# A two-layer hybrid block: gates worked in the product's PSUM bank, output weights split by two other engines, the last weights split during the attention

## The chip, the cores and the metric

The kernel runs on one core of one Trainium2 chip. The metric is the device time of one execution in microseconds, the median of three runs. Engines: PE (TensorE, matmuls), DVE (VectorE), ACT (ScalarE), POOL (GpSimd) and SP (SyncE, which issues most of the DMAs). Each engine works through its own instructions in program order and waits for other engines by semaphores.

## The reference, cut to what matters

Two layers run over 1280 tokens (1024 latent and 256 context) of width 1024, all in fp32. Layer 0 is the part around the first two edits, layer 1's last product the part around the last.

```python
def _ab_mixer(h, ...):                                   # layer 0
    z = h @ w_in
    a, ga, u, v, gb = jnp.split(z, [...])                # 512 columns each
    ya = _multiscale_pool(a, ...) * jax.nn.silu(ga)
    yb = _chunk_sgu(u, v, ...) * jax.nn.silu(gb)
    return jnp.concatenate([ya, yb], axis=-1) @ w_out    # "output product"
x = _layer_norm(ALPHA * x + gate * y, g, b)              # gate = row of silu(c) @ w_mod
...
def _cd_out(f_in, f_gate, attn, d_gate, fnet_w, w_out):  # layer 1
    yc = _fourier_mix(f_in, fnet_w) * jax.nn.silu(f_gate)
    yd = attn * jax.nn.silu(d_gate)                      # attn: 8 heads, 1024 queries, 1280 keys
    return jnp.concatenate([yc, yd], axis=-1) @ w_out    # last product
```

## The kernel before

**Products.** An fp32 operand is kept as two float32r parts, a high one (the value cast) and a low one (value minus high). `split` (L95 on) makes them: the cast is line 106, the subtraction line 107, and its arguments name the engine of each ("s" ACT, "v" DVE, "p" POOL). A product is three matmuls: high·high, high·low, low·high.

**Weights.** `Weights.fetch` loads a weight matrix in pieces of 128x1024 through staging tiles named raw (three buffers, shared with the rows of the modulation weights, rawmm and rawmg, and with other loads) and splits each piece. Without an `eng` entry the cast is DVE's and the subtraction POOL's.

**Order of the program.** A list of deferred work, ordered by a modelled clock, is looked into after each product (`defer`, `tick`, `spread`, `flush`). What is due is written into the program there; `pin` keeps an instruction where it was written. So a change of due times or of a clock moves instructions on every engine.

**Layer 0's gates.** The stages run: pooling input a, its gate ga, v, u, gate gb, output product. The tokens come in three segments (512, 512 and 256 wide). In `t_group`, each product of the gates stands in one of four PSUM banks (tile ps_mm); `ev_ga` and `ev_g` empty it: ACT writes silu of the bank into an SBUF tile (tag h32, two buffers, shared with the temporary tiles of the weighted sums), and DVE multiplies that with y in the tiles S (S5, S6, S7). Beside gb, three weighted sums over the modulation matrix are built: for each of eight rows one load, a DVE multiply-add for the latent row (acc, line 507) and for every second step ACT and POOL for the context row (lines 510 and 511). The last of them gives the gate rows: ps_g (line 530) sums acc over the partitions on PE, and line 532 adds the bias row brg. In the same stretch the first three pieces of the output weights, o0 to o2, are loaded and split (wH_o and wL_o, and wo).

**Output product.** After gb the list is flushed, then `y_split` splits the first two token tiles of y into yhl (the first by DVE alone, the second with POOL), and `y_mm` runs 24 matmuls 128x512 for each tile and half of the columns (ps_o, line 450).

**Attention and the last product.** Eight heads of four blocks follow a string of letters that orders pieces of score products (s), softmax, transposes (pt_p, copied to pT) and value products (av). Letters X take the next piece of a side list: among them `z_step`, which splits the last weights z0 and z1 in pieces 128x512 (cast ACT, subtraction POOL), and `z_piece`, three matmuls of the last product for the first two token tiles. After the attention the other two, z2 and z3, are fetched and split (tile wz), then the gate row and the normalisation vectors are loaded, and the last product (ps_z, line 450) and the final norm run.

```python
sl = hp.tile([P, 512], F32, tag="h32", name="sl", bufs=2)                             # ev_g, L736
nc.scalar.activation(sl[:, :n], ps, AF.Silu)
nc.vector.tensor_mul(y, sl[:, :n].rearrange("p (t c) -> p t c", c=P), y)
```

Of the kernel before, what the change touches and what calls it, by code (L numbers as in the profile page):

```python
# [50 lines left out]
def _body(nc, tc, A, ctx):  # L51
# [429 lines left out]
    for n in range(4):  # L481
        W.add(f"o{n}", halves_of(A["ab_w_out"], n // 2 * 512)[n % 2], 4, 512, eng=(None, None, None, ("s", "v"))[n])
# [146 lines left out]
    for ch in (1, 0):  # L629
        wh, wl = W.use(f"a{ch}")  # L630
        if ch == 1:
            aux(A["ab_pool_w"].rearrange("(g c) d -> c g d", c=P), 4, P, pwH, pwL, "pw")
        pads = [pp.tile([P, PADW], F32, tag="pad", name=f"pad{ch}"), spare[:, 0:PADW]]
        for pd in pads:
            for a0 in (0, 8 + S, PADW - 8):
                nc.gpsimd.memset(pd[:, a0:a0 + 8], 0.0)

        def ev_a(sg, j, ps, pads=pads):
            nc.scalar.copy(pads[j][:, OFF[sg]:OFF[sg] + SEG[sg][1]], ps)

# [12 lines left out]
        def ev_ga(sg, j, ps, ch=ch):  # L653
            g = 2 * ch + j
            y, pv, n = y_of(sg, g), ps.rearrange("p (t c) -> p t c", c=P), SEG[sg][1]
            if (sg, g) in half_done:
                sl = hp.tile([P, 512], F32, tag="h32", name="slg", bufs=2)[:, :n]
                nc.scalar.activation(sl, ps, AF.Silu)
                nc.vector.tensor_mul(y, sl.rearrange("p (t c) -> p t c", c=P), y)
            else:  # L660
                nc.scalar.activation(y, pv, AF.Silu)
            half_done.add((sg, g))

        t_group(wh, wl, h0, K0, ev_ga)
# [4 lines left out]
    sv = pool("sv", stack=st1)  # L669
# [4 lines left out]
    acc2 = sv.tile([P, 2, D], F32, name="acc2")  # L674
# [37 lines left out]
    def ev_v(t, ps):  # L712
# [8 lines left out]
           3.5, 12.0)  # L721
    for ch in range(2):
        wh, wl = W.use(f"u{ch}")

        def ev_u(sg, j, ps, ch=ch):
            y = y_of(sg, 4 + 2 * ch + j)
            pin(nc.vector.tensor_mul(y, ps.rearrange("p (t c) -> p t c", c=P), y))

        t_group(wh, wl, h0, K0, ev_u)
    for ch in range(2):  # L730
        wh, wl = W.use(f"gb{ch}")

# [82 lines left out]
    yh = {0: y_split(0), 1: y_split(1)}  # L815
    ps_of = {}
    for t in range(NT):
        src = A["x"][t * P:(t + 1) * P, :] if t < NL else A["ctx"][(t - NL) * P:(t - NL + 1) * P, :]
        if t == 0:
# [8 lines left out]
            wo.append(W.use("o3", ahead=False))  # L828
        xt = wp.tile([P, D], F32, tag="raw", name=f"xr{t}", bufs=3)
# [278 lines left out]
    def q_piece(hd, qq):  # L1108
# [64 lines left out]
    st5 = ExitStack()  # L1173
    ap_ = pool("ap", side="right", stack=st5)
# [76 lines left out]
    def s_piece(i, j):  # L1251
# [174 lines left out]
    yz, st_f = dict(enumerate(tail["y"])), tail["stack"]  # L1426
# [158 lines left out]
```

## Time and profile before

| what | value |
|---|---|
| time, median of 3 runs | 1096.69 us (1096.38 to 1096.76) |
| profiled execution: its own time | 1095.3 us |
| its span | 1093.5 us |
| mean granted clock | 0.992 of full speed |
| PE busy | 1061.9 us (97%) |
| DVE / ACT / POOL busy | 746.5 / 482.3 / 514.5 us (68 / 44 / 47%) |

The span is what the trace covers; 1.8 us of the profiled execution lie around it. Busy times of PE overlap each other by the pipeline, so what PE loses is seen in its idle stretches, and in the granted clock, which the page gives as a share of full speed.

### The profile page before, as it was taken

To read this page: it belongs to the slowest core of one execution; us is meant where nothing else is said; L and a number is where in the kernel's file an instruction comes from. 1 tells how busy PE (TensorE), PEld (TensorE's weight loads), DVE (VectorE), ACT (ScalarE), POOL (GpSimd) and SP (SyncE) were. 2 spreads that over 40 slices of the span, in tenths; PEclk is the share of its full clock that TensorE was granted. 3 is DMA by queue.
4 is the path that set the end of the run, shared out by engine and by line. 5 is a ranking of instruction groups with operands and counts; after the bars stand their busy time and mean duration, and the time that the engine had idled before them with its cause. 6 is when DMAs were issued, how large, how long until landed. Compare 5 with 4: busy or idle time off the path is not lost.

```text
span 1093.5 us, 16754 instructions
## 1 busy us (share of the span) xinstructions
PE 1061.9 (97%) x6082; PEld 912.0 (83%) x6082; DVE 746.5 (68%) x1664; ACT 482.3 (44%) x1145; POOL 514.5 (47%) x457
## 2 busy tenths in 40 slices
PE   8999999999988999999999999999999999999996
PEld 6888888888866888898888887889989989897886
DVE  3672646789986666777220056898999989894776
ACT  3511234523311333542021144788888888995010
POOL 3561401354482343122293125675655664875872
PEclk9999999999998999999999999999999999999999
DMA  9720110245442322502322010000000002014221
GB/s 365 248 76 29 49 58 1 78 140 184 141 165 90 109 97 93 153 1 92 121 77 77 25 58 29 2 1 1 1 1 1 1 1 59 20 59 153 98 102 73
DMA packets 39059, 85.61 MB, mean 78 GB/s; under 512 B 3056, under 2 KB 17520, under 8 KB 38080
## 3 DMA queue, kind: packets, MB, share of 16 engines
q1 hardware_dynamic: 36160, 76.60, 21.5%
q0 software_dynamic: 1664, 5.84, 1.4%
q10 hardware_dynamic: 1152, 2.10, 0.5%
q8 instruction: 48, 0.79, 0.3%
q14 instruction: 35, 0.29, 0.1%
HBM read 76.13 MB, written 8.39 MB: 77 GB/s over the span
## 4 chain that ended last, share of the span: by engine, by line
PE 73%; DVE 14%; DMA 4%; ACT 3%; issue 3%; POOL 3%; SPq 0%; DVEq 0%; POOLq 0%; ACTq 0%
PE ps_mm L210 16%; PE ps_o L450 10%; PE s L1106 8%; PE ps_n L450 8%; PE ps_z L450 7%; PE av L1324 5%; PE pt_p L1299 5%; DVE acc L507 3%; PE acc L362 2%; PE ps_y L1059 2%; PE ps_c L210 2%; PE pq L1116 1%; DVE S L507 1%; DVE mx L1265 1%; DMA rawmm<-in_cd_w_mod 1%
## 5 line engine op out<-in xcount | busy, mean ns | idle before, releaser
L1106 PE MATMUL s<-kT,qT 96*128 96x512 f32 (+1 forms) x576 | 147.8, 370 | 2.7 <-ACT p L1277 1.6
L1277 ACT ACTIVATE p<-s,mx 128x512 f32<-128x512 f32 (+1 forms) x192 | 119.0, 625 | 13.4 <-DVE mx L1288 12.5
L1265 DVE TENSOR_REDUCE mx<-s 128x1 f32<-128x512 f32 (+1 forms) x192 | 112.2, 595 | 10.6 <-PE s L1106 8.6
L1308 DVE TENSOR_TENSOR pT<-pt_p,pT 128x512 fp32r<-128x512 f32 x160 | 108.2, 684 | 11.4 <-ACT pT L1304 9.2
L1285 POOL TENSOR_SCALAR p<-p,mx 128x1280 f32<-128x1280 f32 x64 | 85.6, 1341 | 39.9 <-ACT pT L1304 11.2
L1106 PEld LDWEIGHTS s<-kT,qT 96*128 96x128 f32 x576 | 90.7, 189 | 15.5 <-ACT p L1277 5.3
L1304 ACT CAST pT<-pt_p 128x512 fp32r<-128x512 f32 x160 | 92.8, 588 | 19.1 <-PE pt_p L1299 11.9
L1299 PE MATMUL pt_p<-ident,p 128*128 128x128 f32 x640 | 93.0, 273 | 0.9 <-DVE kT L1212 0.5
L1299 PEld LDWEIGHTS pt_p<-ident,p 128*128 128x128 f32 x640 | 74.4, 140 | 7.6 <-ACT q L1122 1.1
L1324 PE MATMUL av<-pT,V 128*128 128x256 f32 x480 | 78.6, 291 | 0.1
L1324 PEld LDWEIGHTS av<-pT,V 128*128 128x128 f32 x480 | 67.5, 189 | 4.5 <-DVE pT L1308 0.3
L450 PE MATMUL ps_o<-wH_o,yhl 128*128 128x512 f32 x160 | 55.9, 411 | 6.0 <-DVE yhl L106 5.6
L450 PE MATMUL ps_o<-wo,yhl 128*128 128x512 f32 x240 | 57.5, 392 | 0.0
L450 PEld LDWEIGHTS ps_o<-wo,yhl 128*128 128x128 f32 x240 | 45.1, 189 | 9.2
L450 PE MATMUL ps_n<-wH_v,h 128*128 128x512 f32 x160 | 52.6, 397 | 0.0
L210 PE MATMUL ps_mm<-h,wH_u 128*128 128x512 f32 (+1 forms) x192 | 51.9, 358 | 0.0
L210 PE MATMUL ps_mm<-h,wH_gb 128*128 128x512 f32 (+1 forms) x192 | 51.6, 357 | 0.0
L210 PE MATMUL ps_mm<-h,wH_ga 128*128 128x512 f32 (+1 forms) x192 | 51.2, 354 | 0.0
L710 POOL TENSOR_TENSOR S<-S,bsb 128x256 f32<-128x256 f32 x20 | 18.3, 921 | 66.5 <-DVE S L709 66.5
L450 PE MATMUL ps_z<-wz,yz 128*128 128x512 f32 (+1 forms) x216 | 45.4, 367 | 2.5 <-POOL wz L107 2.5
L450 PEld LDWEIGHTS ps_z<-wz,yz 128*128 128x128 f32 x216 | 37.2, 188 | 9.7 <-POOL wz L107 2.9
L107 POOL TENSOR_TENSOR yhl<-S,yhl 128x1024 fp32r<-128x1024 f32 x9 | 23.5, 2609 | 40.4 <-DVE yhl L106 40.4
(394 smaller groups left out, 2832.8 us busy)
## 6 DMA issues: line engine op xcount, KB each, us to landing
rawmm<-in_cd_w_mod SPq DMA_DIRECT2D x16, 512.0 KB, 3.6
wm<-in_mod SPq DMA_DIRECT2D x7, 1024.0 KB, 9.0
rawmg<-in_ab_w_mod SPq DMA_DIRECT2D x8, 512.0 KB, 3.6
raw_o<-in_ab_w_out SPq DMA_DIRECT2D x8, 512.0 KB, 3.7
xr<-in_x SPq DMA_DIRECT2D x8, 512.0 KB, 3.6
xn_d<-S POOLq DMA_DIRECT2D x8, 512.0 KB, 2.9
rawmg<-in_cd_w_mod SPq DMA_DIRECT2D x8, 512.0 KB, 4.5
raw_z<-in_cd_w_out SPq DMA_DIRECT2D x8, 512.0 KB, 3.8
```

The source lines that it names most:

```text
L107: keep((nc.gpsimd if l == "p" else nc.vector).tensor_sub(dL, src, _f(dH)))
L210: nc.tensor.matmul(out, lhsT=a, rhs=b, start=(i == 0), stop=(i == n - 1))
L450: nc.tensor.matmul(ps, lhsT=lhsT(a, kk), rhs=w[b][:, k, :], start=(kk + i == 0), stop=(kk == KT - 1 and i == 2))
L507: pin(nc.vector.scalar_tensor_tensor(o, raw[:, c], s, o, op0=ALU.mult, op1=ALU.add))
L1106: pin(nc.tensor.matmul(out, lhsT=a, rhs=b, start=(i == 0), stop=(i == 2)))
L1265: pin(nc.vector.tensor_reduce(out=mx[:, j:j + 1], in_=ps, axis=AX.X, op=ALU.max))
L1277: pin(nc.scalar.activation(p32[:, e0:e0 + en], sc[e], AF.Exp, bias=mx[:, 3:4], scale=1.0, accum_out=mx[:, 4 + e:5 + e]))
L1285: pin(nc.gpsimd.tensor_scalar(p32, p32, mx[:, 8:9], 1.0, op0=ALU.mult, op1=ALU.mult))
L1299: pin(nc.tensor.transpose(pt[:, kk * 256 + i * P:kk * 256 + (i + 1) * P], P_of[2 * B + i][:, k * P:(k + 1) * P], ident))
L1304: pin(nc.scalar.copy(pT_of[B, kp][:, 0, :], pt))
L1308: pin(nc.vector.tensor_sub(pT[:, 1, :], pt, _f(pT[:, 0, :])))
L1324: pin(nc.tensor.matmul(av, lhsT=vv, rhs=pT[:, hl, kk * 256:(kk + 1) * 256], start=(k == 0 and hl == 0), stop=(k == NT - 1 and hl == 1)))
```

## The change

The changed kernel does four things. The Silu of layer 0's gates is written back into the product's bank, and DVE multiplies out of it. The output weights o0 to o2 are split by ACT (cast) and DVE (subtraction). The first two token tiles of y are split inside gb's last group, as deferred work, cast by ACT and subtracted by DVE; for that the pool of their tiles opens earlier, and the flush stands behind the first products; the distance of the weighted sums' steps is 3.4 where it was 3.5. The last weights z2 and z3 are loaded and split in the attention in pieces of 128x512 (ACT and POOL), into a slot that is free there and into the query tiles after the last score product's use.

```diff
@@ -481 @@ output weights
-        W.add(f"o{n}", halves_of(A["ab_w_out"], n // 2 * 512)[n % 2], 4, 512, eng=(None, None, None, ("s", "v"))[n])
+        W.add(f"o{n}", halves_of(A["ab_w_out"], n // 2 * 512)[n % 2], 4, 512, eng=("s", "v"))
@@ ev_ga
-                sl = hp.tile([P, 512], F32, tag="h32", name="slg", bufs=2)[:, :n]
-                nc.scalar.activation(sl, ps, AF.Silu)
-                nc.vector.tensor_mul(y, sl.rearrange("p (t c) -> p t c", c=P), y)
+                nc.scalar.activation(ps, ps, AF.Silu)
+                nc.vector.tensor_mul(y, pv, y)
@@ weighted sums
-           3.5, 12.0)
+           3.4, 12.0)
@@ gb
+    st_v.close()
+    st2 = ExitStack()
+    lp = pool("lp", stack=st2)
+    yh = {}
+
+    def y_split(t):
+        yhl = lp.tile([P, 2, KT, P], F32R, tag="yhl", name=f"yhl{t}", bufs=2)
+        split(yhl[:, 0], yhl[:, 1], Y[t // 4][:, t % 4], "s" if t < 2 else "v", "p" if t > 1 else "v")
+        yh[t] = yhl
...
-            sl = hp.tile([P, 512], F32, tag="h32", name="sl", bufs=2)
-            n = SEG[sg][1]
-            nc.scalar.activation(sl[:, :n], ps, AF.Silu)
-            nc.vector.tensor_mul(y, sl[:, :n].rearrange("p (t c) -> p t c", c=P), y)
+            nc.scalar.activation(ps, ps, AF.Silu)
+            nc.vector.tensor_mul(y, ps.rearrange("p (t c) -> p t c", c=P), y)
...
+            for t in range(2):
+                defer(3.5 + 5.0 * t, lambda t=t: y_split(t))
         t_group(wh, wl, h0, K0, ev_g, (1, 2))
-    flush()
...
-    def y_split(t):
-        yhl = lp.tile([P, 2, KT, P], F32R, tag="yhl", name=f"yhl{t}", bufs=2)
-        split(yhl[:, 0], yhl[:, 1], Y[t // 4][:, t % 4], "v", "p" if t else "v")
-        return yhl
...
-    yh = {0: y_split(0), 1: y_split(1)}
...
             wo.append(W.use("o3", ahead=False))
+            flush()
@@ attention
+    def z_room(n):
+        if n == 2:
+            hl = slot(keep, 0, [P, 2, 2048], F32R, "wz2")
+            z2.extend((hl[:, 0], hl[:, 1]))
+        W.fetch(f"z{n}", 1e9, dst=z2)
+
     def z_step(i):
...
+        if i == 12:
+            w["hl"] = [qp.tile([P, 2048], F32R, tag="qT", name=f"wz3{c_}", bufs=2).rearrange("p (k n) -> p k n", k=4)
+                       for c_ in "HL"]
...
+    put("X", lambda: z_room(2), lambda: count["A"] >= (NB - 6) * NT // 2)
+    for i in range(8, 12):
+        put("X", lambda i=i: z_step(i), lambda: count["A"] >= (NB - 5) * NT // 2)
+    put("X", lambda: z_room(3), lambda: W.state["z2"]["todo"] is not None and W.state["z2"]["todo"][1][2] == 2)
+    for i in range(12, 16):
+        put("X", lambda i=i: z_step(i), lambda: count["r"] == HEADS * NL)
@@ after the attention
-    for n in (2, 3):
-        hl = fin.tile([P, 2, 2048], F32R, name=f"wz{n}")
-        W.state[f"z{n}"]["eng"] = (("s", "v"), ("s", "p"))[n - 2]
-        W.fetch(f"z{n}", 1.0 + 4.0 * (n - 2), 1.0, dst=(hl[:, 0, :], hl[:, 1, :]))
```

The due times move instructions. PE before, the end of gb's second segment (h_2, h_3: pieces of its tokens) and the start of the third (h_4), with ps_g, the sums of acc over the partitions, between them:

```order
L210 MATMUL ps_mm<-h_3_123,wH_gb_2548 128x512 x2
L210 MATMUL ps_mm<-h_3_123,wL_gb_2549 128x512
L210 MATMUL ps_mm<-h_2_122,wH_gb_2548 128x512 x2
L210 MATMUL ps_mm<-h_2_122,wL_gb_2549 128x512
L530 MATMUL ps_g<-acc_1323,ones 128x512 x4
L210 MATMUL ps_mm<-h_4_124,wH_gb_2548 128x256 x2
```

PE now, the same place:

```order
L210 MATMUL ps_mm<-h_3_123,wH_gb_2558 128x512 x2
L210 MATMUL ps_mm<-h_3_123,wL_gb_2559 128x512
L530 MATMUL ps_g<-acc_1313,ones 128x512 x4
L210 MATMUL ps_mm<-h_3_123,wH_gb_2558 128x512 x2
L210 MATMUL ps_mm<-h_3_123,wL_gb_2559 128x512
L210 MATMUL ps_mm<-h_3_123,wH_gb_2558 128x512 x2
L210 MATMUL ps_mm<-h_3_123,wL_gb_2559 128x512
L210 MATMUL ps_mm<-h_3_123,wH_gb_2558 128x512 x2
L210 MATMUL ps_mm<-h_3_123,wL_gb_2559 128x512
L210 MATMUL ps_mm<-h_2_122,wH_gb_2558 128x512 x2
```

The four ps_g stand twelve matmuls of the second segment earlier; the gate's products themselves keep their order.

DVE before, the same stretch up to the first output product (acc is the weighted sum, S_93 to S_95 the tiles of y, wo and wL_o parts of output weights, yhl the split tiles of y):

```order
L738 TENSOR_TENSOR S_93<-sl,S_93 128x4x128
L106 CAST wo_2899<-raw_o_0_2900 128x1024
L507 SCALAR_TENSOR_TENSOR acc_1323<-rawmg_2888,scv,acc_1323 128x512 x2
L106 CAST wo_2899<-raw_o_2_2902 128x1024
L738 TENSOR_TENSOR S_94<-sl,S_94 128x4x128
L106 CAST wo_2904<-raw_o_0_2905 128x1024
L106 CAST wo_2904<-raw_o_2_2907 128x1024
L738 TENSOR_TENSOR S_94<-sl,S_94 128x4x128
L532 TENSOR_TENSOR S_95<-ps_g,brg_2981 128x512 x4
L106 CAST yhl_3055<-S_93 128x1024
L106 CAST yhl_3058<-S_93 128x1024
L107 TENSOR_TENSOR yhl_3055<-S_93,yhl_3055 128x1024
```

DVE now:

```order
L746 TENSOR_TENSOR S_93<-ps_mm,S_93 128x4x128
L507 SCALAR_TENSOR_TENSOR acc_1313<-rawmg_2845,scv,acc_1313 128x512 x4
L507 SCALAR_TENSOR_TENSOR acc_1313<-rawmg_2867,scv,acc_1313 128x512 x2
L746 TENSOR_TENSOR S_93<-ps_mm,S_93 128x4x128
L107 TENSOR_TENSOR wo_2903<-raw_o_0_2904,wo_2903 128x1024
L107 TENSOR_TENSOR yhl_2936<-S_93,yhl_2936 128x1024
L107 TENSOR_TENSOR yhl_2978<-S_93,yhl_2978 128x1024
L107 TENSOR_TENSOR wo_2903<-raw_o_2_2906,wo_2903 128x1024
L746 TENSOR_TENSOR S_94<-ps_mm,S_94 128x4x128
L107 TENSOR_TENSOR wo_2908<-raw_o_0_2909,wo_2908 128x1024
L107 TENSOR_TENSOR wo_2908<-raw_o_2_2911,wo_2908 128x1024
L532 TENSOR_TENSOR S_95<-ps_g,brg_2962 128x512 x4
```

The casts have left DVE and subtractions of weights have come to it; the subtractions of both first tiles yhl stand ahead of the last weights and of the gate rows (L532), where the casts and the first tile's subtraction stood behind L532 and the second tile's was POOL's.

ACT before, from the last copies of the attention (pT, transposed softmax; o, head output; yz, the last product's left side; wz, z2 and z3):

```order
L1304 CAST pT<-pt_p 128x512 x3
L1338 COPY o<-av 64x256
L106 CAST wz_10373<-raw_z_0_10374 128x1024
L106 CAST wz_10373<-raw_z_2_10376 128x1024
L106 CAST wz_10378<-raw_z_0_10379 128x1024
L106 CAST yz_10442<-fg 128x512
L106 CAST yz_10442<-dg 128x512
L106 CAST yz_10504<-fg 128x512
L106 CAST yz_10504<-dg 128x512
```

ACT now:

```order
L1309 CAST pT<-pt_p 128x512 x4
L106 CAST wz3H<-raw_z_0_10087 128x512
L1309 CAST pT<-pt_p 128x512
L1343 COPY o<-av 64x256
L1309 CAST pT<-pt_p 128x512
L106 CAST wz3H<-raw_z_0_10087 128x512
L1309 CAST pT<-pt_p 128x512
L106 CAST wz3H<-raw_z_2_10089 128x512
L1309 CAST pT<-pt_p 128x512
L106 CAST wz3H<-raw_z_2_10089 128x512
L1343 COPY o<-av 64x256
```

The four casts 128x1024 of z2 and z3 (the last stands behind the yz) have left the stretch behind the attention. As 128x512 casts, the four of z3 stand between the last casts of pT, and four of z2 further ahead.

## Rows read from the trace of the kernel before

**Rows 1.** The page, busy time: us, share of the span, instructions

```profile
PE 1061.9 (97%) x6082; PEld 912.0 (83%) x6082; DVE 746.5 (68%) x1664; ACT 482.3 (44%) x1145; POOL 514.5 (47%) x457
```

**Rows 2.** What PE waited for, summed: us, times, longest

```profile
PE ps_o L450 <- DVE yhl L106: 5.6, 1, 5.6
PE ps_z L450 <- POOL wz L107: 2.5, 1, 2.5
```

**Rows 3.** Timeline of PE, gates to output product: start, us, instructions, idle before

```profile
311.85 0.61 PE L210 MATMUL ps_mm<-h,wH_gb 128*128 128x512 f32 x2
...
317.18 2.84 PE L530 MATMUL ps_g<-acc,ones 128*128 128x512 f32 x6 [1.59 <-DVE acc L507]
...
325.49 0.28 PE L210 MATMUL ps_mm<-h,wL_gb 128*128 128x256 f32 x1
331.35 0.77 PE L450 MATMUL ps_o<-wH_o,yhl 128*128 128x512 f32 x1 [5.58 <-DVE yhl L106]
...
340.39 0.39 PE L450 MATMUL ps_o<-wH_o,yhl 128*128 128x512 f32 x1
...
341.30 0.39 PE L450 MATMUL ps_o<-wL_o,yhl 128*128 128x512 f32 x1
```

**Rows 4.** Windows: us, busy PE, PEld, DVE, ACT, POOL; PEclk; DMA

```profile
330.00:335.00 5.00, 3.20 (x7) 2.13 (x8) 5.00 (x6) 2.68 (x4) 3.06 (x1) 0.50 0.50 162
335.00:340.00 5.00, 5.00 (x18) 3.96 (x17) 3.06 (x4) 0.00 (x0) 0.17 (x1) 0.71 0.41 116
```

**Rows 5.** Timeline of DVE in the same place

```profile
302.88 3.80 DVE L507 SCALAR_TENSOR_TENSOR acc<-rawmg,scv,acc 128x512 f32<-128x512 f32 x2 [1.81 <-DMA rawmg<-in_ab_w_mod]
306.98 4.43 DVE L507 SCALAR_TENSOR_TENSOR acc<-rawmg,scv,acc 128x512 f32<-128x512 f32 x4 [0.30 <-DMA rawmg<-in_ab_w_mod]
...
313.03 0.68 DVE L106 CAST wo<-raw_o 128x1024 fp32r<-128x1024 f32 x1
313.63 3.50 DVE L507 SCALAR_TENSOR_TENSOR acc<-rawmg,scv,acc 128x512 f32<-128x512 f32 x2
...
322.72 5.49 DVE L738 TENSOR_TENSOR S<-sl,S 128x512 f32<-128x512 f32 x1
...
331.73 1.21 DVE L107 TENSOR_TENSOR yhl<-S,yhl 128x1024 fp32r<-128x1024 f32 x1
```

**Rows 6.** Timeline of POOL, earlier and in the same place

```profile
230.64 3.36 POOL L511 TENSOR_TENSOR acc<-acc,tmp 128x512 f32<-128x512 f32 x2 [1.36 <-DVE acc L507]
...
300.00 6.13 POOL L107 TENSOR_TENSOR wL_o<-raw_o,wH_o 128x1024 fp32r<-128x1024 f32 x2 [5.39 <-DVE wH_o L106]
...
322.94 4.71 POOL L107 TENSOR_TENSOR wo<-raw_o,wo 128x1024 fp32r<-128x1024 f32 x2
```

**Rows 7.** Timeline of DVE beside the first row of the last group

```profile
231.08 0.68 DVE L727 TENSOR_TENSOR S<-ps_mm,S 128x512 f32<-128x512 f32 x1
...
232.01 2.54 DVE L507 SCALAR_TENSOR_TENSOR acc<-rawmm,scv,acc 128x512 f32<-128x512 f32 x2
```

**Rows 8.** Timeline of ACT, in the gates and after the attention

```profile
318.29 0.60 ACT L737 ACTIVATE sl<-ps_mm 128x512 f32<-128x512 f32 x1 [3.93 <-POOL acc L511]
...
1001.87 0.62 ACT L106 CAST yz<-fg 128x512 fp32r<-128x512 f32 x1
...
1005.13 1.05 ACT L106 CAST wz<-raw_z 128x1024 fp32r<-128x1024 f32 x1 [1.08 <-DMA raw_z<-in_cd_w_out]
```

**Rows 9.** Chain that ended last, pieces: start, us, what

```profile
316.61 3.78 DMA raw_o<-in_ab_w_out
...
985.63 0.70 PE ps_z L1400 x3
```

**Rows 10.** Windows in the attention, columns as before

```profile
950.00:960.00 10.00, 9.77 (x65) 8.26 (x64) 7.94 (x20) 9.81 (x27) 10.00 (x10) 1.00 0.33 107
```

**Rows 11.** Timeline of POOL after the attention

```profile
1004.71 1.31 POOL L107 TENSOR_TENSOR yz<-fg,yz 128x512 fp32r<-128x512 f32 x1
...
1009.76 2.36 POOL L107 TENSOR_TENSOR wz<-raw_z,wz 128x1024 fp32r<-128x1024 f32 x1
```

More of the change, by code (lines that the diff above doesn't have):

```diff
@@ L666, in _body @@
     sp_.close()
-    sv = pool("sv", stack=st1)
+    acc2 = pool("sv0", stack=st1).tile([P, 2, D], F32, name="acc2")
+    st_v = ExitStack()
+    sv = pool("sv", stack=st_v)
     ws = sv.tile([P, 4, 2, P], F32R, name="ws")
@@ L673, in _body @@
     nc.gpsimd.dma_start(out=bsb, in_=A["ab_sgu_b"].partition_broadcast(P))
-    acc2 = sv.tile([P, 2, D], F32, name="acc2")
     def v_norm(t, ps):
@@ L845, in _body @@
         if t + 2 < NT:
-            yh[t + 2] = y_split(t + 2)
+            y_split(t + 2)
     st2.close()
+    st1.close()
     halves = [W.use("c0", ahead=False), W.use("c1", ahead=False)]
@@ L1133, in parts @@
             if hd not in qT_of:
-                qT_of[hd] = ap_.tile([DK, 2, S], F32R, tag="qT", name=f"qT{hd}", bufs=2)
+                qT_of[hd] = qp.tile([DK, 2, S], F32R, tag="qT", name=f"qT{hd}", bufs=2)
             qT = qT_of[hd]
@@ L1173, in _body @@
     st5 = ExitStack()
+    st_f = ExitStack()
+    qp = pool("qp", side="right", stack=st_f)
     ap_ = pool("ap", side="right", stack=st5)
@@ L1285, in divide @@
             pin(nc.gpsimd.tensor_scalar(p32, p32, mx[:, 8:9], 1.0, op0=ALU.mult, op1=ALU.mult))
+            count["r"] += 1
         def bias():
@@ L1349, in _body @@
     LEAD = 3
-    count = {"S": 0, "A": 0}
+    count = {"S": 0, "A": 0, "r": 0}
     tail = {}
@@ L1356, in block_end @@
             st_k.close()
-            tail["stack"] = ExitStack()
-            fin0 = pool("fin0", stack=tail["stack"])
+            fin0 = pool("fin0", stack=st_f)
             tail["y"] = [z_split(t, fin0) for t in range(2)]
@@ L1378, in z_load @@
         count["z"] = count["A"] + 3
+    z2 = []
+    def z_room(n):
[3 more added lines that the diff above has]
+        W.fetch(f"z{n}", 1e9, dst=z2)
     def z_step(i):
         w = W.state[f"z{i // 4}"]
+        if i == 12:
+            w["hl"] = [qp.tile([P, 2048], F32R, tag="qT", name=f"wz3{c_}", bufs=2).rearrange("p (k n) -> p k n", k=4)
+                       for c_ in "HL"]
         r, k = i % 4 // 2, i % 4
@@ L1401, in z_piece @@
                                  start=(kk + i == 0), stop=(kk == KT - 1 and i == 2)))
-    put("X", z_load, lambda: len(todo["X"]) == 25 and count["A"] >= (NB - 8) * NT // 2)
+    put("X", z_load, lambda: len(todo["X"]) == 35 and count["A"] >= (NB - 8) * NT // 2)
     for i in range(8):
         put("X", lambda i=i: z_step(i), lambda: count["A"] >= count.get("z", 1e9))
+    put("X", lambda: z_room(2), lambda: count["A"] >= (NB - 6) * NT // 2)
[4 more added lines that the diff above has]
+        put("X", lambda i=i: z_step(i), lambda: count["r"] == HEADS * NL)
     for t in range(2):
@@ L1425, in _body @@
         run("EMNRrTHLAodXxyz")
-    yz, st_f = dict(enumerate(tail["y"])), tail["stack"]
+    yz = dict(enumerate(tail["y"]))
     flush()
```

3 lines of the change are left out of this document (removed).

## Prediction

> **What bounds the kernel now.** I read the page first: PE is busy for 97% of the span [rows 1], so time can come only from places where PE stands idle or runs at a lower clock. Then the sum of what PE waited for: two entries stand out, and both lie where the change works, 5.6 us before the first output product of layer 0 and 2.5 us in the last product [rows 2]. Then the timeline of PE at the first place. The gates of layer 0 issue their last matmul at 325.49, and the first output product starts at 331.35, after an idle of 5.58 that DVE's yhl ended; ahead of that 1.59 were lost before ps_g, which waited for acc [rows 3]. The reader is to see what follows the idle, too: the first 24 matmuls of the output product take from 331.35 to 340.39, 9.04 us, while the four starts from 340.39 to 341.30 are 0.23 apart, by which 24 take 5.46 [rows 3]. The granted clock was 0.50 and 0.71 in these two windows [rows 4], the lower of the two levels (1.2 GHz) for the first, and PE had stood idle before it fell. So the idle costs 5.6 directly and 3.6 behind it.
>
> Why is yhl late? The timeline of DVE, which is full there, shows the reasons in its queue ahead of yhl: waits for loads of rawmg (1.81 and 0.30), sums stretched to 3.50 for two, and one multiply of the gate that took 5.49 [rows 5] beside two POOL subtractions of output weights [rows 6]. The chain of waits adds that a load of an output weight (3.78) stood on the way [rows 9], since its staging buffer came free only after POOL's subtraction; those take 6.13 for two at 300.00 [rows 6].
>
> **The change part by part.** The sum is made against the profiled execution, 1.8 us of which lie outside its span and are taken as unchanged; the median of the runs is 1.4 above that execution, so I subtract the sum from the median.
>
> *Gates in the bank.* No instruction is added: ACT writes to the bank, DVE's multiply reads it. What goes is ACT's wait for a tile that POOL's sums hold (3.93 before one Silu) [rows 8], and a second SBUF operand of DVE. For the price of a multiply out of a bank the trace has a row: 0.68 for 128x512, beside a POOL sum that began before it and took 3.36 for two [rows 6, 7]; the sums that follow, with two SBUF inputs, took 1.27 each beside it [rows 7]. So the multiply of 5.49 should fall to 0.7. The price: a bank is held until DVE has come. Four banks, and a product of 24 matmuls takes 5.46, so a bank is wanted again some 16 us after its product; DVE's latest is a few us. Nothing, from 0 to 1.5. The same edit in ga (where PE loses nothing) I cost at nothing; PE's own work and the same four banks hide it.
>
> The Trainium skill ("SBUF — State Buffer", "Who interferes with whom") says that a DVE instruction with at most one SBUF input does not contend with GpSimd, one with two does, with a GpSimd instruction that reads SBUF. The trace agrees for the multiply, 0.68 against 1.27 [rows 7]. The rule speaks for this edit and against the next.
>
> *Output weights.* Six POOL subtractions (2.4 to 3.1 each) [rows 6] and six DVE casts (0.68) [rows 5] go; ACT gets six casts (1.05) [rows 8] and DVE six subtractions, at 1.21, the duration of yhl's of that size [rows 5]. ACT has the room: it stands idle before its Silu there. DVE gains 6 x 0.53 = 3.2 us of work net, but loses the stretching. From the start of the sums at 302.88 to the last of acc, DVE now has eight sums and a multiply of 128x512 and two subtractions: at 0.68 and 1.21 that is 6.1 + 2.4 = 8.5, end 311.4. At the durations of before (3.80 + 4.43 + 3.50 [rows 5], plus 0.7 and 2.4) it ends at 317.7. POOL keeps only its own sums there, so I take a value near the lower end, 313. By the rule above, the two subtractions, with both inputs in SBUF, would contend with POOL's sums; four of these at 1.7 are left, and were DVE blocked for all of them, acc would come at 318, which is rival (a).
>
> *ps_g.* It moves twelve matmuls ahead: it was due 12 x 0.23 = 2.7 us behind the start at 311.85 [rows 3], and is now due at 311.85 itself. Its first two passes (1.0) need no late acc, so acc at 313 costs 0 to 0.5; I take 0.5 in place of 1.59. Behind ps_g in PE's queue stand all the rest of the gates and the output product, so any more is paid in full.
>
> *First rows.* yhl's casts go to ACT, and the two subtractions (1.21 each) stand in DVE's queue right behind the first multiply after acc and one subtraction of wo. With acc at 313, yhl of the first tile is ready at 313 + 0.7 + 1.2 + 1.2 = 316. PE, whose last gate matmul of 128x256 (half a step, 0.12) starts at 325.49 at the latest and ends by 325.65, now finishes the gates at 325.65 - 1.59 + 0.5 = 324.6. So 8 us of cover. The other things that the first output products need: wL_o, done at 305; wo (the rest of DVE's queue: two more subtractions, a multiply, two subtractions, 6.7, so about 323); and a bank, released by the gates' multiplies behind the gate rows, near 327 and wanted near 330. What is late next is therefore nothing by more than a few us; the bias row that the gate rows wait for is nearest.
>
> So the first 24 matmuls run from 324.6 at the upper clock (2.4 GHz) for 5.46, to 330.1, in place of 340.39: 10.3 us. I take off 0.3 for the shorter waits of PE at the mod vectors' row, which also moved ahead: 10.0. Bounds: 3 (rival a) to 10.9, which is all that is lost there.
>
> *Loads.* With the step 3.4 one more load of the weighted sums stands ahead of gb's weights and of the output weights on SP. That puts the weights one load later, and they are fetched a whole stage of products ahead of their use: nothing, from 0 to 1.
>
> *z2 and z3 in the attention.* Eight casts 128x512 on ACT at 0.62 [rows 8] and eight subtractions on POOL at 1.31 [rows 11]. Where z0 and z1 do the same, ACT and POOL are full (9.81 and 10.00 of 10), and PE lost 0.23 [rows 10]. z2's half I price by that row: 0.4, from 0 to 2.5 (four casts on the path). z3's casts stand between the last casts of pT, where PE waits for these; and two groups of three matmuls of the last product (0.70) [rows 9], which filled such waits, now come later. 0.6, from 0 to 3.9 (2 x 0.7 + 4 x 0.62).
>
> *After the attention.* The wait of 2.5 for POOL's wz [rows 2] goes: its subtraction ended at 1012.1 because four of yz (1.31) stood ahead of it [rows 11]. What is late next are those of yz, for tiles that come 10 us later; and the loads of the vectors, which now find SP free. Gain 2.5; from 1.5 to 2.5.
>
> Sum: -10.0 + 0.4 + 0.6 - 2.5 = -11.5. Forecast 1096.7 - 11.5 = 1085.2, own range 1083.5 to 1088.
>
> **The rivals.**
>
> (a) *The earlier ps_g meets acc as late as before.* For it: the loads of rawmg share buffers with the output weights, now freed by DVE subtractions which stand in the same queue as the sums, and DVE is full. Against it: what made DVE wait was POOL. If acc comes at 317.1, PE waits 4.3 instead of 1.59, the gates end at 325.65 + 2.7 = 328.4, and the clock may fall as it did after 5.58: the first tile ends at 333.8 to 337.4, a gain of 3.0 to 6.6. With the end's 1.5: about 1090.4. The Trainium skill's port rule, if DVE were blocked in full, leads here; no row shows subtractions of this size beside POOL's sums.
>
> (b) *The attention's end pays.* z2 and z3 on the path at their far ends, 2.5 + 3.9, against 2.5 gained: the end costs 3.9, the gates still give 10.0: about 1090.6; with half of that loss, 1087.4.
>
> (c) *Held banks, the slower side.* In the gates ACT freed a bank; now DVE does, in one queue with the sums and with subtractions that wait for loads. If DVE comes to a multiply later than the third product after it, PE stands, and each such stop costs what DVE was late: the worst multiply of before was 5.49 - 0.68 = 4.8 over its own time [rows 5, 7]. gb has twelve products. Two such stops take 9.6 of the 11.5; from the third on (14.4) the change is slower than before; four are 19.2, so 1104.4. Against it: 16 us of cover to each bank, and DVE's longest wait for a load in this stretch is 1.81 [rows 5].
>
> (d) *Nothing that can be measured.* (a) at its worst (3.0 gained) with (b) at its worst (3.9 lost): 1097.6.
>
> **How the numbers follow.** The forecast has 0.62, (a) 0.14, (b) 0.11, (c) 0.06, (d) 0.07. A measurement of this kernel tells 0.2% (2.2 us) from no change. Faster by more: forecast, (a) and (b), 0.87; within: (d), 0.07; slower: (c), 0.06. The range takes in the forecast's own with 0.7 below it (a transition without any loss, 0.9 more), and (a) and (b) above: 1082.8 to 1091.5. The two cases of no gain are left out.
>
> **What would show it.** In the trace of the changed kernel: PE's wait for yhl is gone from the sum of waits, the granted clock is 1.00 from 320 to 345 on, and the 24 matmuls of the first tile stand 0.23 apart right behind the gates. ps_g's wait is below 1; at 4 it is (a). DVE's multiplies from the bank take 0.7 also beside POOL; if they stay at 2 to 5, that step is wrong. DVE's new subtractions take 1.2; at 3 the queue is longer than worked out. Waits of PE for ps_mm banks (released by DVE's multiply) would be (c). The window of z2's steps in the attention loses 0.2 to 0.5 of PE; PE is full from the last av to the final norm, without a wait for wz; if ACT's casts of wz3 stand before a waiting transpose by 2 us or more, it is (b). The forecast is wrong if the output product still starts above 326 of this trace's clock.

## The result, and the profile after

The changed kernel takes 1081.68 us, median of four runs (1081.31 to 1083.06), against 1096.72 in the same comparison: a ratio of 0.9865, 95% interval 0.9848 to 0.9882. That is 15.0 us less, where 11.5 were forecast; the time lies 1.1 below the stated range (1082.8 to 1091.5). Its profiled execution took 1081.9, with a span of 1080.1 against 1093.5, 13.4 less.

What PE waits for, in the changed kernel (us in total, times, longest). These are its two largest entries; the two of [rows 2] and the wait of ps_g for acc are no longer in the list:

```profile
PE pt_c L878 <- DVE z L868: 2.0, 2, 1.6
PE s L1108 <- ACT p L1281: 1.6, 6, 0.3
```

PE at the first place (start, us, instructions, idle before in brackets), which answers to [rows 3]; the last two groups are the start of the product that follows the output product, now and in the kernel before:

```profile
311.88 3.60 PE L530 MATMUL ps_g<-acc,ones 128*128 128x512 f32 x8
...
323.69 0.28 PE L210 MATMUL ps_mm<-h,wL_gb 128*128 128x256 f32 x1
323.81 0.40 PE L450 MATMUL ps_o<-wH_o,yhl 128*128 128x512 f32 x1
...
329.28 0.39 PE L450 MATMUL ps_o<-wH_o,yhl 128*128 128x512 f32 x1
```

```profile
439.86 0.39 PE L450 MATMUL ps_o<-wH_o,yhl 128*128 128x512 f32 x1
440.09 0.35 PE L210 MATMUL ps_c<-wH_c,h 128*128 128x416 f32 x1
```

```profile
451.20 0.35 PE L210 MATMUL ps_c<-wH_c,h 128*128 128x416 f32 x1
```

ps_g runs its eight passes at 311.88 without a wait in brackets, and the output product starts 0.12 behind the last matmul of the gates. Its first 24 matmuls take from 323.81 to 329.28, 5.47 us; before, they took 9.04. The last two groups show the whole gain of the first place: ps_c starts at 440.09 where it started at 451.20. That is 11.1 us.

The windows of that stretch (busy time of PE, PEld, DVE, ACT and POOL; granted clock; DMA), which answer to [rows 4]:

```profile
320.00:325.00 5.00, 5.00 (x40) 4.78 (x39) 1.91 (x5) 1.48 (x3) 0.00 (x0) 1.00 0.45 156
325.00:330.00 5.00, 5.00 (x24) 4.14 (x23) 3.19 (x4) 2.46 (x3) 0.00 (x0) 1.00 0.45 137
330.00:335.00 5.00, 5.00 (x24) 4.14 (x23) 1.64 (x4) 0.00 (x0) 0.00 (x0) 1.00 0.20 76
```

PE is full and the clock stays at its upper level. DVE in the same place, which answers to [rows 5]:

```profile
297.19 2.11 DVE L507 SCALAR_TENSOR_TENSOR acc<-rawmg,scv,acc 128x512 f32<-128x512 f32 x2
...
303.01 5.10 DVE L507 SCALAR_TENSOR_TENSOR acc<-rawmg,scv,acc 128x512 f32<-128x512 f32 x6 [0.82 <-DMA rawmg<-in_ab_w_mod]
308.03 0.68 DVE L746 TENSOR_TENSOR S<-ps_mm,S 128x512 f32<-128x512 f32 x1
308.63 1.71 DVE L107 TENSOR_TENSOR wo<-raw_o,wo 128x1024 fp32r<-128x1024 f32 x1
310.27 2.35 DVE L107 TENSOR_TENSOR yhl<-S,yhl 128x1024 fp32r<-128x1024 f32 x2
...
314.28 2.52 DVE L107 TENSOR_TENSOR wo<-raw_o,wo 128x1024 fp32r<-128x1024 f32 x2
318.38 2.48 DVE L532 TENSOR_TENSOR S<-ps_g,brg 128x512 f32<-128x512 f32 x4 [1.58 <-DMA brg<-in_ab_b_mod]
```

The last six sums of DVE come in one row of 5.10 and end at 308.1; in the kernel before the last two ended at 317.1. The two sums ahead of these six were done by 299.3; in the kernel before they started at 302.88 [rows 5]. Both tiles of yhl are subtracted by 312.6, 11 us before PE asks for them. The multiply out of the bank takes 0.68 at 308.03, beside a POOL sum that ran from 305.97 to 309.26. What DVE waits for now is the bias row brg (1.58), and nothing hangs on that.

The windows at the attention's end, where the splits of z2 and z3 now stand (columns as above; [rows 10] has one of before):

```profile
950.00:960.00 10.00, 10.00 (x73) 9.19 (x72) 8.97 (x25) 9.68 (x25) 7.16 (x7) 1.00 0.16 53
960.00:970.00 10.00, 10.00 (x69) 8.87 (x68) 8.71 (x21) 9.59 (x26) 9.09 (x9) 1.00 0.52 173
970.00:980.00 10.00, 9.94 (x80) 9.22 (x78) 8.06 (x18) 8.91 (x23) 7.45 (x7) 1.00 0.83 297
980.00:990.00 10.00, 9.85 (x60) 8.38 (x59) 4.01 (x8) 7.93 (x15) 8.99 (x8) 1.00 0.02 6
```

PE loses 0.06 and 0.15 in the last two windows, and nothing in the window before, where ACT is 96% busy and three of z2's four casts stand; the kernel before loses 0.23 and 0.05 from 980 to 1000. Measured by where PE's rows stand, the attention's start and the last score product are both 10.8 earlier than before: z2's splits cost PE nothing. The span ends 13.4 earlier, the wait for wz gone.

### The profile page after: what moved, and what is told of

Same layout as the page of the kernel before. It is cut to its first block, busy times and chain, and to the rows that moved or that the text cites. A ratio compares the mean times of both kernels' runs of the same rounds, so it can differ in the third digit from the quotient of the medians.

```text
span 1080.1 us, 16762 instructions
## 1 busy us (share of the span) xinstructions
PE 1059.1 (98%) x6082; PEld 910.8 (84%) x6082; DVE 734.2 (68%) x1661; ACT 489.1 (45%) x1157; POOL 497.7 (46%) x456
## 4 chain that ended last, share of the span: by engine, by line
PE 81%; DVE 7%; ACT 4%; DMA 3%; issue 3%; POOL 2%; SPq 0%; DVEq 0%; POOLq 0%; ACTq 0%
PE ps_mm L210 25%; PE ps_o L450 10%; PE ps_n L450 8%; PE s L1108 8%; PE ps_z L450 7%; PE av L1329 5%; PE pt_p L1304 5%; DMA S<-in_xT 2%; PE ps_y L1061 2%; PE ps_c L210 2%; PE pq L1118 2%; ACT p L1281 2%; DVE mx L1269 1%; ACT pT L1309 1%; PE ps_z L1416 1%
## 5 line engine op out<-in xcount | busy, mean ns | idle before, releaser
L210 PE MATMUL ps_c<-wH_c,h 128*128 128x416 f32 (+1 forms) x160 | 42.3, 341 | 0.0
L107 POOL TENSOR_TENSOR yhl<-S,yhl 128x1024 fp32r<-128x1024 f32 x8 | 20.3, 2532 | 45.2 <-DVE yhl L106 45.2
L1281 ACT ACTIVATION_READ_ACCUMULATOR p<-s,mx 128x1 f32 x192 | 39.8, 207 | 0.0
```

The costliest lines, as they stand in the source:

```text
L210: nc.tensor.matmul(out, lhsT=a, rhs=b, start=(i == 0), stop=(i == n - 1))
L1281: pin(nc.scalar.activation(p32[:, e0:e0 + en], sc[e], AF.Exp, bias=mx[:, 3:4], scale=1.0, accum_out=mx[:, 4 + e:5 + e]))
```

## The experiments

In the labels, u stands for the changed kernel with one part undone, p for the kernel before with one part alone. Each median has beside it that of the kernel before on the same chip, 1096.8 for the first eight and 1096.25 for the last four.

| run | median us | ratio to before, 95% interval |
|---|---|---|
| c_before | 1096.92 | 0.9999 (0.9990 to 1.0007) |
| u_z | 1085.54 | 0.9892 (0.9877 to 0.9907) |
| u_bank | 1082.51 | 0.9865 (0.9851 to 0.9878) |
| u_wo | 1082.76 | 0.9868 (0.9854 to 0.9881) |
| p_bank | 1092.64 | 0.9963 (0.9949 to 0.9978) |
| p_wo | 1087.86 | 0.9916 (0.9896 to 0.9935) |
| p_ysplit | 1086.63 | 0.9908 (0.9893 to 0.9923) |
| u_ysplit2 | 1082.67 | 0.9869 (0.9854 to 0.9885) |
| p_pool | 1087.45 | 0.9915 (0.9901 to 0.9930) |
| p_z | 1092.17 | 0.9958 (0.9946 to 0.9971) |
| best_fi | 1080.62 | 0.9853 (0.9840 to 0.9866) |
| best_fi_sp | 1080.85 | 0.9856 (0.9843 to 0.9870) |

**c_before**, no edit: what the kernel before does from run to run.

> The kernel before, unchanged, run again: its profiled execution took 1095.3 us (span 1093.5, mean granted clock 0.992), 1.4 below the median of its timed runs, and the changed kernel's profiled execution is 0.2 above its own median. Theory A: the unprofiled runs of the kernel before spend one more piece of the trace's clock steps (3.4 us) at the lower level behind the 5.58 us idle, so they show spans of 1094.6 to 1095.3 and a mean clock of 0.990 to 0.991, and the new profile shows where. Rival B: the span is 1093.5 in every run, and the 1.4 lie outside it, before or behind the program. Rival C: the start differs by chance, by as much in the changed kernel; then spans scatter by 1.5 both ways around 1094.5.

Its eleven runs went from 1095.14 to 1098.07, with spans of 1093.3 to 1096.3, so rival B is out: the scatter lies inside the span. Its profile, of a run of 1097.96, shows one place that theory A did not name. Windows behind the wait for wz, first this run, then the profile of before:

```profile
1010.00:1015.00 5.00, 2.50 (x11) 1.70 (x10) 0.26 (x1) 0.00 (x0) 5.00 (x3) 0.96 0.50 206
1015.00:1020.00 5.00, 5.00 (x17) 3.97 (x16) 2.39 (x5) 0.00 (x0) 4.92 (x3) 0.70 0.00 0
```

```profile
1010.00:1015.00 5.00, 2.83 (x12) 2.35 (x13) 0.70 (x1) 0.00 (x0) 4.92 (x3) 1.00 0.30 121
1015.00:1020.00 5.00, 5.00 (x23) 4.13 (x23) 2.49 (x4) 0.00 (x0) 4.92 (x3) 1.00 0.11 28
```

The 29 matmuls behind that wait, in this run and in the profile of before:

```profile
1013.25 8.51 PE L450 MATMUL ps_z<-wz,yz 128*128 128x512 f32 x29 [2.50 <-POOL wz L107]
```

```profile
1012.17 6.89 PE L450 MATMUL ps_z<-wz,yz 128*128 128x512 f32 x29 [2.50 <-POOL wz L107]
```

Here the clock fell behind the 2.5 us idle (0.70 in the second window); in the profile read for the prediction it did not. It costs 1.6 (8.51 against 6.89). Behind the 5.58 idle both profiles have the same stretch at the lower clock. The first 50 us differ by 0.75 too, so rival C has a part.

**u_z**, the last weights undone:

```diff
-    put("X", lambda: z_room(2), lambda: count["A"] >= (NB - 6) * NT // 2)
...
-        put("X", lambda i=i: z_step(i), lambda: count["r"] == HEADS * NL)
...
     fin = pool("fin", stack=st_f)
+    for n in (2, 3):
+        hl = fin.tile([P, 2, 2048], F32R, name=f"wz{n}")
+        W.state[f"z{n}"]["eng"] = (("s", "v"), ("s", "p"))[n - 2]
+        W.fetch(f"z{n}", 1.0 + 4.0 * (n - 2), 1.0, dst=(hl[:, 0, :], hl[:, 1, :]))
```

> The changed kernel with z2 and z3 fetched and split behind the attention again. Theory A: the wait for wz comes back (2.5 us) and nothing in the attention is saved, since the casts there cost PE nothing: 1084.2 (1083.7 to 1084.7), PE's wait for POOL wz 2 to 3 us. Rival B: the splits in the attention cost about 1, which is saved: 1083.2. Rival C: with the rest of the kernel earlier, the wait is gone anyway: 1081.7.

3.9 more than the changed kernel by the medians, 3.0 by the ratios, above theory A's 2.5. Its profiled run is 4.9 longer in span: 1.0 is there already at 52 us, before any edit; the wait is back with 2.5; and the rest is the clock, which fell behind it:

```profile
PE ps_z L450 <- POOL wz L107: 2.5, 1, 2.5
```

```profile
1000.00:1005.00 5.00, 2.78 (x7) 2.20 (x8) 0.24 (x1) 0.00 (x0) 4.92 (x3) 0.70 0.29 118
```

**p_z**, the change's edits of z2 and z3 alone in the kernel before:

> The kernel before with z2 and z3 in the attention, and nothing else. Theory A: the wait for wz (2.5 us) goes, and with it the chance that the clock falls behind it, which costs 1.6 in some runs of the kernel before: median 1093.0 to 1094.0, fastest run 1092.2, and no step at the lower clock between 900 and 1070. Rival B: a start that differs by chance makes the scatter of the kernel before, the clock behind wz is no part: 1094.3, with the same scatter of 3.7 as before.

4.1 to 4.6 us by the medians of the kernel before beside it (1096.25) and in the earlier comparisons (1096.8), more than the wait of 2.5. All five runs lie from 1091.61 to 1092.33, a scatter of 0.7 against 3 in the kernel before beside it. That this is the clock's doing alone is not shown: the changed kernel has no wait for wz either, and its four runs scatter by 1.8. Its windows in the same place:

```profile
1000.00:1010.00 10.00, 10.00 (x46) 8.29 (x45) 2.10 (x3) 0.00 (x0) 9.92 (x6) 1.00 0.00 0
1010.00:1020.00 10.00, 10.00 (x46) 8.25 (x45) 9.32 (x23) 0.20 (x1) 6.44 (x4) 1.00 0.29 97
```

No idle, no lower clock: theory A, 0.8 under its range. So the wait cost 2.5 always and about 1.6 more where the clock fell. Of the seven profiled executions that have it, the four with a fallen clock are c_before, u_z, p_wo and p_pool, and the three without are before, p_bank and p_ysplit: the 29 matmuls behind the wait take 8.34 to 8.51 in the four and 6.87 to 6.89 in the three.

**u_bank, u_wo, u_ysplit2**: each of the three parts in the gates undone by itself. u_ysplit2 puts back the place of the call and the engines of yhl's split; the earlier pool, the later flush and the step 3.4 stay in it, as they do in the other two.

```diff
# u_bank (ev_g, and likewise ev_ga)
-            nc.scalar.activation(ps, ps, AF.Silu)
+            sl = hp.tile([P, 512], F32, tag="h32", name="sl", bufs=2)
+            nc.scalar.activation(sl[:, :n], ps, AF.Silu)
# u_wo
-        W.add(f"o{n}", halves_of(A["ab_w_out"], n // 2 * 512)[n % 2], 4, 512, eng=("s", "v"))
+        W.add(f"o{n}", halves_of(A["ab_w_out"], n // 2 * 512)[n % 2], 4, 512, eng=(None, None, None, ("s", "v"))[n])
# u_ysplit2
-        split(yhl[:, 0], yhl[:, 1], Y[t // 4][:, t % 4], "s" if t < 2 else "v", "p" if t > 1 else "v")
+        split(yhl[:, 0], yhl[:, 1], Y[t // 4][:, t % 4], "v", "p" if t else "v")
...
-                defer(3.5 + 5.0 * t, lambda t=t: y_split(t))
         t_group(wh, wl, h0, K0, ev_g, (1, 2))
...
+    for t in range(2):
+        y_split(t)
     ps_of = {}
```

> The changed kernel with the gates' Silu into SBUF tiles again. Theory A: the queue of POOL subtractions was the root, the tile only its victim: POOL has just its sums there now, the multiplies take 0.7 to 1.8 and the output product starts without a wait: 1081.7 to 1083. Rival B: the multiply out of SBUF (5.49 before) and ACT's wait for the tile are the root: DVE is late by 4 to 5 us, PE stands before the output product and the clock falls: 1087 to 1091.

> The changed kernel with o0 to o2 cast by DVE and subtracted by POOL again. Theory A: the chain of POOL subtraction, load, sum comes back: acc at 317 and ps_g, due at 311.9, waits 4 to 5 us, weights are late, clock falls: 1087 to 1092. Rival B: the place of yhl's split in DVE's queue is what counts, POOL's lateness is covered: below 1083.7.

> The changed kernel with yhl's split written where it was, behind gb's last group, by DVE alone for the first tile and DVE and POOL for the second. Theory A: the other two parts make DVE early enough: no wait before the output product, 1081.7 to 1083. Rival B: yhl's casts on DVE and its place are needed: the wait comes back with 2 to 5 us and the clock falls: 1085 to 1090.

None of them costs more than 1.1 us by the medians, or 0.4 by the ratios, whose intervals overlap with the changed kernel's, so no cost is shown; and in all three the wait before the output product stays away. Theory A of u_wo fell; with POOL's subtractions back, DVE's casts are stretched beside them, but yhl's subtraction stands among them and comes in time (DVE in u_wo):

```profile
303.49 7.13 DVE L507 SCALAR_TENSOR_TENSOR acc<-rawmg,scv,acc 128x512 f32<-128x512 f32 x6 [1.79 <-DMA rawmg<-in_ab_w_mod]
...
315.24 1.21 DVE L107 TENSOR_TENSOR yhl<-S,yhl 128x1024 fp32r<-128x1024 f32 x1
316.37 2.88 DVE L106 CAST wo<-raw_o 128x1024 fp32r<-128x1024 f32 x1
319.18 1.22 DVE L107 TENSOR_TENSOR yhl<-S,yhl 128x1024 fp32r<-128x1024 f32 x1
...
323.72 2.47 DVE L532 TENSOR_TENSOR S<-ps_g,brg 128x512 f32<-128x512 f32 x4
```

The cast of 128x1024 takes 2.88 here, 0.68 alone [rows 5].

In u_ysplit2 the call stands behind the gates again, and yhl's first cast still runs at 311.63, ahead of the gate rows (DVE in u_ysplit2):

```profile
311.63 0.69 DVE L106 CAST yhl<-S 128x1024 fp32r<-128x1024 f32 x1
```

So the place of the call is not what put yhl early, and this run does not show that the bank and the weights are enough without the earlier pool. No run takes that pool out of the changed kernel.

**p_bank, p_wo, p_ysplit**: each part by itself, the same edits of the change in the kernel before; p_ysplit has the earlier pool, the later flush and the step 3.4 with it.

> The kernel before with one part alone: the Silu of the gates back into the bank, DVE's multiply out of it. Theory A: three things stood in DVE's queue ahead of yhl (the multiply of 5.49, loads held by POOL's subtractions, yhl's own place), and each alone gives a part: the multiply falls to 0.7, yhl is ready about 5 us earlier, the wait before the output product falls from 5.6 to 0 to 2 and the clock holds: 1088 to 1092. Rival B: POOL's chain of subtraction, load and sum alone sets the time, so less than 2 us: 1095 to 1097. Rival C: any one part is enough for all of the gain in the gates: 1085 to 1087.

> The kernel before with one part alone: o0 to o2 cast by ACT and subtracted by DVE. Theory A: the loads no longer wait for POOL, the multiply of 5.49 has no POOL subtraction beside it, but DVE has 3 us more of work ahead of yhl: the wait before the output product falls to 0 to 3: 1087 to 1092. Rival B: DVE's added work and ACT's wait for the tile eat it: 1095 to 1098. Rival C: all of the gates' gain: 1085 to 1087.

> The kernel before with one part alone: yhl's split inside gb's last group (ACT and DVE), with its pool opened earlier, the flush behind the first products and the step 3.4, so that ps_g is due at 311.9 here too. Theory A: yhl comes off the end of DVE's queue, but acc is still late by POOL's chain: ps_g waits 2 to 5 us at its earlier place, the output product starts without a wait of its own: 1087 to 1092. Rival C: all of the gates' gain: 1085 to 1087. Rival D: the wait only moves, from yhl to acc and to the banks: 1094 to 1097.

The bank alone gives 4.1, 0.6 short of theory A's range: the wait for yhl falls to 2.4, and the clock still falls (windows of p_bank):

```profile
PE ps_o L450 <- DVE yhl L106: 2.4, 1, 2.4
```

```profile
325.00:330.00 5.00, 2.07 (x5) 1.36 (x6) 5.00 (x8) 1.84 (x3) 2.96 (x2) 0.75 0.72 257
330.00:335.00 5.00, 5.00 (x14) 3.89 (x14) 3.48 (x3) 1.81 (x2) 0.94 (x1) 0.56 0.37 107
```

The weights alone give 8.9 (theory A): PE waits 0.17 and 0.94, and the clock holds. yhl's place alone, with its pool, gives 10.2, rival C's answer; acc, due early there too, made PE wait 0.48 (PE in p_ysplit):

```profile
312.68 1.02 PE L530 MATMUL ps_g<-acc,ones 128*128 128x512 f32 x2
314.18 2.84 PE L530 MATMUL ps_g<-acc,ones 128*128 128x512 f32 x6 [0.48 <-DVE acc L507]
...
325.38 0.40 PE L450 MATMUL ps_o<-wH_o,yhl 128*128 128x512 f32 x1
```

So the parts do not add up: 4.1 + 8.9 + 10.2 is twice the 11.1 that was to be had. The bank and the weights shorten the queue ahead of yhl, whose first cast still stands behind the gate rows in both runs (326.28 and 324.07); the third part moves yhl ahead of the gate rows. The weights alone, or yhl's place alone, leave PE about a microsecond to lose in this stretch or less, so a second part has little to take.

**p_pool**: what put yhl last? In p_ysplit the pool of its tiles was opened earlier, together with the call. Here only the pool's place is changed; for that the pool of ws and bsb closes there, and acc2, the tile of acc, gets a pool of its own.

```diff
+    acc2 = pool("sv0", stack=st1).tile([P, 2, D], F32, name="acc2")
+    st_v = ExitStack()
-    sv = pool("sv", stack=st1)
+    sv = pool("sv", stack=st_v)
-    acc2 = sv.tile([P, 2, D], F32, name="acc2")
...
+    st_v.close()
+    st2 = ExitStack()
+    lp = pool("lp", stack=st2)
     for ch in range(2):
         wh, wl = W.use(f"gb{ch}")
...
     flush()
-    st1.close()
-    st2 = ExitStack()
-    lp = pool("lp", stack=st2)
...
     st2.close()
+    st1.close()
```

> The kernel before with one line's place alone: the pool of yhl's tiles is opened ahead of gb (the pool with ws and bsb closed there, acc2 in a pool of its own), while y_split, its engines, the flush, the step 3.5 and all else stay. By the order of the program, the first yhl's cast and subtraction then stand ahead of the last two weights' casts, of both multiplies of S_94 and of the gate rows. Theory A: the memory of the tile, not the place of the call or the engines, held yhl back: before, it lay where the weighted sum was, and its first write had to stand behind the last reader. Then the wait for yhl is gone, as with any one of the other parts: ps_g's wait of 1.6 stays, 1086 to 1089. Rival B: DVE's multiply of 5.49 and POOL's queue now hold the banks and the weights instead: 1090 to 1094.

8.8 to 9.4 us by one edit that moves no call of a computation: theory A. The wait of ps_g stays (1.4). DVE in p_pool, then PE at the start of the output product, then DVE in the kernel before:

```profile
312.97 3.50 DVE L507 SCALAR_TENSOR_TENSOR acc<-rawmg,scv,acc 128x512 f32<-128x512 f32 x2
316.40 1.75 DVE L106 CAST yhl<-S 128x1024 fp32r<-128x1024 f32 x1
...
318.67 1.21 DVE L107 TENSOR_TENSOR yhl<-S,yhl 128x1024 fp32r<-128x1024 f32 x1
...
326.63 2.88 DVE L742 TENSOR_TENSOR S<-sl,S 128x512 f32<-128x512 f32 x1
329.44 2.47 DVE L532 TENSOR_TENSOR S<-ps_g,brg 128x512 f32<-128x512 f32 x4
```

```profile
324.96 0.40 PE L450 MATMUL ps_o<-wH_o,yhl 128*128 128x512 f32 x1
```

```profile
330.52 1.28 DVE L106 CAST yhl<-S 128x1024 fp32r<-128x1024 f32 x2
```

yhl's first cast starts at 316.40, as soon as the sums are done, and its subtraction at 318.67; in the kernel before they were at 330.52 and 331.73. The last multiply of S_94 takes 2.88 (5.49 before), the gate rows end at 331.9, 1.3 later than before, and PE waits for neither. In the program of before, yhl's first cast waits for the last sums into acc and for the load of bsb: its tile lay in the memory of the pool that held these. By the trace these sums were over by 318.3 (the last is POOL's), and the cast ran at 330.52; what held it from there on was its place in DVE's queue. So the memory worked through the order of the program. How that order follows from it is not shown; that it goes with the pool's place is: in the five profiles with the late pool (before, c_before, p_z, p_bank, p_wo) yhl's first cast stands behind the gate rows, in all others yhl stands ahead of them.

**best_fi, best_fi_sp**: one more weight, in the same manner. In the changed kernel PE still waits 1.1 for wL_fi from POOL, and a subtraction of 128x128 on DVE takes 2.51 beside POOL's, then 0.29:

```profile
494.20 2.51 DVE L107 TENSOR_TENSOR cL<-zt,cH 128x128 fp32r<-128x128 f32 x1
...
496.89 0.29 DVE L107 TENSOR_TENSOR cL<-zt,cH 128x128 fp32r<-128x128 f32 x1
```

```diff
-   W.add(f"fi{ch}", halves_of(w1, c0)[ch], 4, 512, eng=None if ch else ("s", "v"))
+   W.add(f"fi{ch}", halves_of(w1, c0)[ch], 4, 512, eng=("s", "v"))       # best_fi; ("s", "p") for fi1 in best_fi_sp
```

> The changed kernel, and the weight fi1 (second half of the Fourier input's weights) cast by ACT and subtracted by DVE as the others are. In the changed kernel PE is idle for 1.3 us from 490 to 510, waits for wL_fi from POOL for 1.1, and one DVE subtraction of 128x128 takes 2.51 beside POOL's subtraction of fi1 where its neighbour takes 0.29. Theory: the wait goes: 0.8 to 1.3 less, 1080.4 to 1080.9. Rival: the wait moves to DVE's added subtraction: 1081.7.

> The same weight cast by ACT, subtracted by POOL. Theory (it is POOL's subtraction beside DVE's that is slow, and its length of 2.4 to 2.5 that PE waits for): 0 to 0.5 less, 1081.2 to 1081.7. Rival (DVE's cast, behind its queue, is what comes late): as good as the other variant, 1080.4 to 1080.9.

1080.62 is below the changed kernel's 1081.68 (which ran beside another set of runs of the kernel before, and the intervals of the two ratios overlap; the traces show the gain). PE's wait for wL_fi has left the list, and PE is idle for 0.23 in these 20 us, where it was for 1.33 (windows of best_fi, then of the changed kernel):

```profile
490.00:500.00 10.00, 9.77 (x45) 7.75 (x44) 8.40 (x26) 3.30 (x9) 0.74 (x1) 1.00 0.30 83
500.00:510.00 10.00, 10.00 (x46) 8.28 (x45) 6.75 (x11) 1.76 (x3) 0.00 (x0) 1.00 0.86 293
```

```profile
490.00:500.00 10.00, 9.12 (x40) 7.00 (x39) 9.38 (x21) 0.83 (x3) 5.29 (x3) 1.00 0.18 53
500.00:510.00 10.00, 9.55 (x42) 7.92 (x43) 6.57 (x10) 1.77 (x3) 0.40 (x1) 1.00 0.73 240
```

The variant with POOL is as good, so it was the cast behind DVE's queue that came late, not POOL's length.

## Why the prediction was wrong

The two places and the way of the change came out, none of the rivals did, and the size was too small by 3.5 us. Term by term, from the traces:

| term | forecast | measured in the trace |
|---|---|---|
| gates and first output product | -10.0 | -11.1 |
| waits of PE behind it, to the attention | 0 | +0.3 |
| z2 in the attention | +0.4 | 0.0 |
| z3 and the moved pieces at its end | +0.6 | 0.0 |
| wait for wz | -2.5 | -2.5 |
| sum | -11.5 | -13.4 |
| median against the profiled execution | 0 | -1.6 |

The measured terms are rounded; their sum is the difference of the spans. Two sizes were off, 1.9 in the terms of the sum and 1.6 in its last line; either alone would have left the time inside the stated range, at 1083.3 or 1083.6, though the first lies 0.2 below the forecast's own range.

**The steps that failed** are two. The terms of the sum were mis-sized: the gates, -10.0 where -11.1 was measured, and z2 and z3, +1.0 together where nothing was lost; they are taken up below. The largest single miss is the sentence "I subtract the sum from the median": it took the 1.4 by which the median of before stood above its profiled execution for a constant. It was not; the changed kernel's profiled execution stands 0.2 above its median. c_before, u_z and p_z show the largest part of what it was: behind the wait for wz the clock falls in some executions, for about 1.6, and the one profile that I had read was of an execution in which it did not. The idle of 2.5 so was worth up to 4.1; u_z measures 3.0 to 3.9 and p_z 4.1 to 4.6, starts that differ by up to 1 included. The rest of the scatter, at the start, is in both kernels and was not followed further.

**Gates.** The clock, the wait and the end of DVE's delay came as forecast: first 24 matmuls 5.47 (5.46), no wait for yhl, the clock at 1.00. The term was mis-sized by 1.1, since I took 0.5 for ps_g and 0.3 for the row of the mod vectors, and both are zero: acc was done at 308.1, not 313. I had counted eight sums from 302.88 on with two subtractions among them; there were six, with none, since two were done by 299.3. The loads held by POOL's subtractions are one part of this: with these back (u_wo) the gap ahead of the six is 1.79, where it is 0.82, and they take 7.13, where they take 5.10, so acc is done at 310.6. The gain even passed the bound of 10.9 by 0.2. Of the 3.6 that I put behind the idle, 0.45 was a second wait, for yhl's subtraction; and the 6.7 of DVE's later queue is 5.5 by the same rows. Neither moves the forecast.

**The reason for yhl's lateness** was half right. What I named (loads, stretched sums, the multiply of 5.49, POOL's subtractions) did stand ahead of yhl in DVE's queue; p_bank and p_wo show that taking it away helps by 4.1 and 8.9. But I read the queue's order as given by the call's place. p_pool and u_ysplit2 show that it went with the pool of the tile. The earlier pool was described as a means for the move; by itself it gives 8.8 to 9.4, as much as the weights by themselves (8.9), and neither the engines nor the deferred call were needed for it.

**The port rule.** The Trainium skill ("SBUF — State Buffer", "Who interferes with whom") names casts among the instructions of DVE that can contend with GpSimd, besides those with two SBUF inputs; the prediction had left the casts out. The runs agree: a cast of 0.68 takes 2.88 beside a POOL subtraction in u_wo, a subtraction of 0.29 takes 2.51 in the changed kernel, and the multiply out of the bank stays at 0.68. The part of the rule that I held against the change, DVE's added subtractions beside POOL's sums, cost little: 1.71 instead of 1.21 for one of them, which met the last of the two sums that POOL had there (305.97 to 309.26).

**Attention.** ACT at 96% and POOL at 91% cost nothing, since PE found other work; the bounds of 2.5 and 3.9 were never near. The 0.23 that I took the price from [rows 10] belongs to the steps of z0 and z1, in both kernels.

## What to carry to other kernels

When an engine's queue puts a late-needed split behind everything else, look for what its destination's memory was used for before: here, moving the opening of one pool gave about 9 us by itself, where all edits of the gates together gave 11. Parts that clear the same queue do not add up; test them alone and one at a time removed before crediting any, and look whether a removal takes out all that came with the part (u_ysplit2 kept the pool). And before subtracting a sum from a median, compare the profiled execution with the median: a gap of that kind can belong to the wait that is about to go.

## What was not expected of the hardware

The same idle of PE, 2.5 us at the same place, was followed by a lower granted clock (0.69 or 0.70 as the mean of a stretch of 5 us) in four profiled executions and not in three; behind 5.6 us it fell in each of the three that had it (before, c_before, p_z), and behind 2.4 in p_bank. A fall behind the 2.5 us idle cost 1.5 to 1.6 us in each of the four, almost two thirds of the idle itself.
